# Pairs of up-projection chunks by seven products, and the down-projection in K=512 groups between them

## The chip, the core and the metric

The kernel runs on one core of one Trainium2 chip. The metric is the device time of one execution in microseconds. A time is the median of several runs; the profile shows one more execution, taken by the hardware profiler. TensorE (PE) multiplies, VectorE (DVE) and ScalarE (ACT) do the elementwise work, GpSimd (POOL) nearly nothing, and SyncE (SP) issues the transfers from main memory. Each works through its own queue in a fixed order.

## The reference

One layer of a hybrid decoder for 544 tokens (512 prompt, 8 x 4 sample), width 1024, in fp32. The change touches the output projection and what follows it:

```
merged = gates[:, :, 0] * ret_out + gates[:, :, 1] * conv_out + gates[:, :, 2] * xa_out
x = x + merged @ w_out                                   # 1024 x 1024
h2 = _rmsnorm(x, g_ffn)
x = x + jnp.square(jax.nn.relu(h2 @ w_up)) @ w_down      # 1024 x 4096, 4096 x 1024
y = _rmsnorm(x, g_final)
```

## The kernel before

An fp32 product is three matmuls of a rounded type: each factor is cast to a high part, the difference is the low part, and hi·hi, hi·lo and lo·hi are summed in a PSUM bank. Activations lie with channels on the 128 partitions and the 544 tokens along the free axis, in two halves of 272.

All projections go through one sequence of **chunks** (`seq`). A chunk is 128 output columns; with a depth of K=1024 it has 8 blocks of 128 x 3 products x 2 halves = 48 matmuls of 272 columns, with K=512 it has 24. `step(t)` issues the matmuls of chunk t (L200) into `pp`, a tile of two banks with two buffers, then `prep(t+2)`, which makes the weight parts of the chunk after next (ScalarE casts `whi` from `raw`, L177; VectorE forms `wlo`, through the helper at L102), then the evacuation of chunk t, then the functions posted for it by `at(key, d, fn)`, and last `load(t+4)`, which issues a DMA from SP into `raw` (two buffers, L166). A raw tile of K=1024 is 512 KB; a **half tile**, K=512, is 256 KB.

The sequence ends with: eight chunks of the output projection (**wo**), whose evacuation (`evac_out`) adds the input `xin` to give the residual `x1` and makes the high and low parts `h2h`, `h2l` of x1 times the gain; four **groups** of eight **up** chunks and eight **down** chunks (`dn`), where group g's down chunks take the 1024 channels that its up chunks have made (`ah`, `al`) and add into x1; in the fourth group the down chunks take only the first 512 channels, and 16 chunks of 12 matmuls (**last**) take the others, one half of the tokens at a time. The weights of last are resident: loaded early into `wres` (L850) and split by `resident`. In the end `final` sums the squares (`fsq`, `sq` into `fin`, L880 and L881) and the output is scaled.

`ffn_scale`, posted behind wo, makes `rs2` = 1/(mean square + eps), with a reciprocal of 544 columns on VectorE. `evac_up` uses it: r = max(p, 0) · rs2 and r · p on VectorE, then a cast on ScalarE and the low part on VectorE (`split`, L114 and L102).

What sets the order: the program is written step by step, and each engine's queue has its instructions in the order in which the code issues them.

Of the kernel before, what the change touches and what calls it, by code (L numbers as in the profile page):

```python
# [21 lines left out]
NB = 8  # L22
# [30 lines left out]
UPD3 = 1  # L53
PE_NS = dict(xa1=(4500, 3), xa2=(1100, 3), xa3=(4500, 3), xa4=(220, 1), ret_k=(1100, 3), ret_scores=(3200, 4),
# [12 lines left out]
class Builder:  # L67
    def __init__(self, ctx, tc, a, o):
        self.tc, self.nc, self.a, self.o = tc, tc.nc, a, o
        self.sb = ctx.enter_context(tc.tile_pool(name="sb", bufs=1))  # L70
        self.ps = ctx.enter_context(tc.tile_pool(name="ps", bufs=1, space=bass.MemoryType.PSUM))
# [6 lines left out]
        self.quota = 99  # L78

# [7 lines left out]
    def tmp(self, s, n=T, dt=F32):  # L87
        return self.sb.tile([P, n], dt, name=self.name(s), tag="T", bufs=NT)

    def small(self, s, dt=F32):  # L90
        return self.sb.tile([P, 2 * P], dt, name=self.name(s), tag="U", bufs=3)

    def const(self, s, shape, dt=F32):
        return self.sb.tile(shape, dt, name=s, tag=s)
# [59 lines left out]
    def load(self, t):  # L154
        if t >= len(self.chunks) or "parts" in self.chunks[t]:
            return
        w, idx = self.chunks[t]["w"]
        ks = self.chunks[t]["ks"]
        if w == "w_mem_kv" and idx % 6 > 1:
            if idx % 2 == 0:  # L160
                self.pair = self.sb.tile([P, 2, 2, 4, P], F32, name=self.name("raws"), tag="S8", bufs=2)
# [7 lines left out]
    def prep(self, t):  # L169
        if t >= len(self.chunks) or "parts" in self.chunks[t]:  # L170
            return
# [15 lines left out]

    def step(self, t):
        c = self.chunks[t]
        self.quota = c.get("quota", 99)  # L190
# [3 lines left out]
        xh, xl = c["rhs"]()  # L194
        n, nk = c["n"], 4 * len(c["ks"])
        for k in range(nk):
            wh, wl = parts[k // 4][0][:, k % 4], parts[k // 4][1][:, k % 4]
            for w, x in ((wh, xh), (wh, xl), (wl, xh)):
                for s in c["hs"]:
                    mm(pt[:, s, :n], w, x[:, 4 * c["ks"][0] + k, s * n:(s + 1) * n],  # L200
                       start=(k == 0 and w is wh and x is xh),
                       stop=(k == nk - 1 and w is wl))
        self.pe_ns += self.pe_cost(t)
        self.dve_ns = max(self.dve_ns, self.pe_ns)
        posts = self.posts.pop(t, [])
# [34 lines left out]
    # ---------------------------------------------------------------- memory keys and values  # L240
# [18 lines left out]
    # ---------------------------------------------------------------- memory attention  # L259
# [25 lines left out]
    def load_s8(self, src, key):  # L285
        t = self.sb.tile([P, 4, 2, 256], F32, name=self.name("s8"), tag="S8", bufs=2)
# [3 lines left out]
    def xa1(self, h):  # L290
# [15 lines left out]
        def tail():  # L306
            for w in range(2):
                self.load_s8(self.a["cmv"][h, w], ("v", w))
            mx = self.sb.tile([P, 6], F32, name=self.name("mx"), tag="mx", bufs=1)
            nm = self.sb.tile([P, 6], F32, name=self.name("nm"), tag="nm", bufs=1)  # L310
            sm = self.sb.tile([P, 6], F32, name=self.name("sm"), tag="sm", bufs=1)
            rs = self.sb.tile([P, 6], F32, name=self.name("rs"), tag="rs", bufs=1)
# [5 lines left out]
            p4 = self.sb.tile([P, 4, NM], F32, name=self.name("p"), tag="P5")  # L318
            ps = self.sb.tile([P, NM], F32, name=self.name("psm"), tag="OS")
# [34 lines left out]
    def xa3(self, h):  # L354
# [14 lines left out]
        def tail():  # L369
# [7 lines left out]
            self.os = self.sb.tile([P, 256], F32, name=self.name("os"), tag="OS")  # L377
# [25 lines left out]
    # ---------------------------------------------------------------- conv branch  # L403
# [6 lines left out]
    def evac_gt(self, c):  # L410
        def f(pt):
# [4 lines left out]
            e = self.sb.tile([P, EXT + SEQ + NB * XS], F32, name=self.name("ext"), tag="ext", bufs=2)  # L416
# [11 lines left out]
    def queue_conv(self, c, e, es):  # L428
# [14 lines left out]
        def sample():  # L443
            cwb = self.vecs[:, w0:w0 + CW].unsqueeze(1).to_broadcast([P, NB, CW])
            r = self.sb.tile([P, NS, NB], F32, name=self.name("cr"), tag="cr", bufs=1)
# [9 lines left out]
        def total():  # L455
            if c == 0:
                self.ysum = self.sb.tile([P, T], F32, name="ysum", tag="ysum")
# [10 lines left out]
    # ---------------------------------------------------------------- retention  # L468
# [48 lines left out]
    def stack_k(self, src):  # L517
        self.kdup = self.small("kdup").rearrange("p (c s) -> p c s", c=2)
        self.kcat = self.small("kcat", F32R).rearrange("p (c s) -> p c s", c=2)
        t = self.sb.tile([P, 2, TS], F32, name=self.name("ks"), tag="ks", bufs=1)  # L520
# [36 lines left out]
    def ret_k(self, h):  # L557
        b = self.to_tokens(self.kf, self.kcat)

        def tail():  # L560
# [5 lines left out]
            self.kst = self.sb.tile([P, 2, 256], F32R, name=self.name("kst"), tag="pk")  # L566
# [44 lines left out]
    def ret_intra_s(self, h):  # L611
# [6 lines left out]
        def tail():  # L618
            self.scs = self.sb.tile([P, P], F32, name=self.name("scs"), tag="scs")
# [3 lines left out]
    def ret_o(self, h):  # L623
# [16 lines left out]
        def tail():  # L640
            self.on = self.sb.tile([P, 4, 256], F32, name=self.name("on"), tag="P5")
            self.os = self.sb.tile([P, 256], F32, name=self.name("os"), tag="OS")
            st = self.sb.tile([P, 5, 6], F32, name=self.name("st"), tag="st", bufs=1)
            mv = self.sb.tile([P, 5, 2], F32, name=self.name("mv"), tag="mv", bufs=1)
            rs = self.sb.tile([P, 5], F32, name=self.name("rsg"), tag="rsg", bufs=1)
# [11 lines left out]
            nb = self.sb.tile([P, 5], F32, name=self.name("nb"), tag="nbg", bufs=1)  # L657
# [56 lines left out]
    # ---------------------------------------------------------------- tail of the mixer  # L714
# [19 lines left out]
    def ln_mean(self):  # L734
# [3 lines left out]
        def tail():  # L738
# [3 lines left out]
            self.vsum = self.sb.tile([P, T], F32, name="vsum", tag="ysum")  # L742
# [57 lines left out]
    def evac_out(self, j):  # L800
        def f(pt):
            if j == 0:
                self.x1 = self.big("x1", [P, NC8, T])
                self.h2h = self.big("h2h", [P, NC8, T], F32R)
                self.h2l = self.big("h2l", [P, NC8, T], F32R)
                self.ssq = self.sb.tile([P, T], F32, name="ssq", tag="ysum")
            self.tt(self.two(self.x1[:, j]), pt[:, :, :HALF], self.two(self.xin[j]), ALU.add)
            gf = self.vec("g_ffn", j)
            self.act(self.h2h[:, j], self.x1[:, j], AF.Copy, scale=gf)
            sq = self.ssq if j == 0 else self.tmp("sq")  # L810
            self.act(sq, self.x1[:, j], AF.Square)
            yield
            self.stt(self.h2l[:, j], self.x1[:, j], gf, self.h2h[:, j], ALU.mult, ALU.subtract)
            if j:
                self.tt(self.ssq, self.ssq, sq, ALU.add)
        return f

    def ffn_scale(self):
        b = self.mean_of(self.ssq)

        def tail():
            self.rs2 = self.sb.tile([P, T], F32, name="rs2", tag="cossin")
            for s in range(2):
                self.act(self.rs2[:, s * HALF:(s + 1) * HALF], b[s][:, :HALF], AF.Identity, bias=self.epsc)
            self.v("reciprocal", self.rs2, self.rs2)
            self.act(self.sb.tile([P, 1], F32, name="warm", tag="mx"), self.epsc, AF.Sqrt)
        return tail

    # ---------------------------------------------------------------- feed-forward
    def evac_up(self, g, k):  # L830
        def f(pt):
            if k == 0 and g == 0:
                self.ah = self.big("ah", [P, NC8, T], F32R)
                self.al = self.big("al", [P, NC8, T], F32R)
            r, t = self.tmp("r"), self.tmp("r2")
            ps = pt[:, :, :HALF]
            self.stt(self.two(r), ps, 0.0, self.two(self.rs2), ALU.max, ALU.mult)
            self.tt(self.two(t), ps, self.two(r), ALU.mult)
            yield from self.split(self.ah[:, k], self.al[:, k], t)
# [8 lines left out]
    def resident_load(self, j):  # L848
        self.wres[j] = self.tmp("wres", 512)
        self.nc.sync.dma_start(out=self.wres[j], in_=self.a["w_down"][24 + j][:, 4:8].rearrange("p k c -> p (k c)"))  # L850

    def resident(self, j):
        w = self.wres[j]
        if j == 0:
            self.rh = self.big("rh", [P, NC8, 4, P], F32R)
            self.rl = {}
        if j % 4 == 0:
            self.rl[j // 4] = self.sb.tile([P, 4, 4, P], F32R, name=self.name("rl"), tag="S8", bufs=2)

        return lambda: self.split(self.rh[:, j], self.rl[j // 4][:, j % 4], w.rearrange("p (k c) -> p k c", k=4))  # L860

    def evac_last(self, s, j):
        def f(pt):
# [5 lines left out]
            if j == 0:  # L869
                if s == 0:  # L870
                    self.fsqt = self.sb.tile([P, T], F32, name="fsq", tag="ysum")
# [39 lines left out]
    # ---------------------------------------------------------------- everything  # L911
    def build(self):
# [6 lines left out]
        memt = self.sb.tile([P, 2, D], F32, name="memt", tag="S8", bufs=2)  # L919
# [337 lines left out]
```

## Time and profile before

| | |
|---|---|
| median of 3 runs | 1159.74 us (1159.67 to 1160.41) |
| span of the profiled execution | 1157.8 us |
| TensorE matmul busy | 1144.7 us (99%), 9292 matmuls |
| VectorE busy | 765.5 us (66%), 1304 instructions |
| ScalarE busy | 450.9 us (39%), 885 instructions |
| mean granted TensorE clock | 0.998 of full |
| DMA | 142.6 MB, 123 GB/s |

The profile is of one execution and its span goes from the first to the last instruction; the runs' time holds something around it as well. A busy share is a mean over the whole span. The row of an instruction has its line in the code, the engine, the operation, output<-inputs by the program's names, and the shape.

### The profile page before, as it was taken

Reading aid. Unit: us, or ns where it says so; the run is one execution under the profiler, and the core shown is the slowest. Engines: PE = TensorE matmul, PEld = TensorE weight load, DVE = VectorE, ACT = ScalarE, POOL = GpSimd, SP = SyncE. Lnnn points to the kernel's source line nnn. Section 1 sums busy time; section 2 is a strip of 40 time slices with the busy share of each in tenths; the row PEclk is TensorE's granted clock in tenths of the full one; section 3 lists DMA queues with packets and bytes.
Section 4 is the critical chain, followed back from the end, with each engine's and each line's share of the span. In section 5 each row is a group of like instructions: output and inputs, shape, how many; then the busy total and the mean of one; then the engine's idle time right before and its main releaser. Section 6 shows DMA issues by size and latency. Waiting matters only on the chain.

```text
span 1157.8 us, 22201 instructions
## 1 busy us (share of the span) xinstructions
PE 1144.7 (99%) x9292; PEld 1120.3 (97%) x9292; DVE 765.5 (66%) x1304; ACT 450.9 (39%) x885; POOL 1.6 (0%) x8
## 2 busy tenths in 40 slices
PE   8999999999999999999999999999999999999996
PEld 8999999999999999999999999999999999999996
DVE  5747898568888988888764766565335435534656
ACT  7735653534343452334454623433223222222322
POOL 0000000000000000000000000000000000000000
PEclk9999999999999999999999999999999999999999
DMA  8555454442215422632522334322222222222402
GB/s 318 189 181 204 161 202 155 169 152 91 78 56 171 170 66 95 223 87 86 188 87 65 99 120 165 127 79 92 92 91 86 82 89 92 92 91 72 153 32 78
DMA packets 42804, 142.60 MB, mean 123 GB/s; under 512 B 4784, under 2 KB 11056, under 8 KB 39632
## 3 DMA queue, kind: packets, MB, share of 16 engines
q1 hardware_dynamic: 42416, 141.01, 36.0%
q8 instruction: 73, 1.20, 0.4%
q14 instruction: 27, 0.22, 0.1%
q10 hardware_dynamic: 288, 0.17, 0.1%
HBM read 126.17 MB, written 15.00 MB: 122 GB/s over the span
## 4 chain that ended last, share of the span: by engine, by line
PE 98%; DVE 1%; ACT 0%; DMA 0%; issue 0%; DVEq 0%; ACTq 0%
PE pp L200 87%; PE xo L365 1%; PE ro L637 1%; PE xs L302 1%; PE tk L551 1%; PE up L701 0%; PE rs L142 0%; PE rs L141 0%; PE rs L140 0%; PE ro L141 0%; PE ro L142 0%; PE ro L140 0%; DMA memt<-in_mem 0%; PE rst L141 0%; PE rst L142 0%; PE rst L140 0%
## 5 line engine op out<-in xcount | busy, mean ns | idle before, releaser
L102 DVE TENSOR_TENSOR wlo<-raw,whi 128x512 fp32r<-128x512 f32 x324 | 220.8, 690 | 280.1 <-ACT whi L177 258.2
L177 ACT CAST whi<-raw 128x512 fp32r<-128x512 f32 x324 | 198.5, 620 | 431.5 <-PE pp L200 403.3
L200 PE MATMUL pp<-hh,whi 128*128 128x272 f32 x1280 | 268.1, 291 | 0.0
L200 PE MATMUL pp<-hl,whi 128*128 128x272 f32 x1280 | 263.9, 288 | 0.0
L200 PE MATMUL pp<-hh,wlo 128*128 128x272 f32 x1280 | 263.3, 287 | 0.0
L200 PEld LDWEIGHTS pp<-hh,whi 128*128 128x128 f32 x1280 | 199.8, 188 | 6.3 <-issue 4.9
L200 PEld LDWEIGHTS pp<-hh,wlo 128*128 128x128 f32 x1280 | 201.1, 188 | 0.0
L200 PEld LDWEIGHTS pp<-hl,whi 128*128 128x128 f32 x1280 | 200.2, 188 | 0.0
L200 PE MATMUL pp<-h2h,whi 128*128 128x272 f32 x512 | 105.8, 288 | 0.0
L200 PE MATMUL pp<-h2l,whi 128*128 128x272 f32 x512 | 105.6, 287 | 0.0
L200 PE MATMUL pp<-h2h,wlo 128*128 128x272 f32 x512 | 105.4, 287 | 0.0
L200 PE MATMUL pp<-ah,whi 128*128 128x272 f32 x448 | 92.4, 288 | 0.0
L200 PE MATMUL pp<-al,whi 128*128 128x272 f32 x448 | 92.4, 288 | 0.0
L200 PE MATMUL pp<-ah,wlo 128*128 128x272 f32 x448 | 92.2, 287 | 0.0
L102 DVE SCALAR_TENSOR_TENSOR y<-ext,vecs,y 128x512 f32<-128x512 f32 x120 | 89.8, 748 | 2.9 <-ACT y L111 2.8
L102 DVE SCALAR_TENSOR_TENSOR odd<-ext,vecs,odd 128x512 f32<-128x512 f32 x112 | 83.6, 747 | 0.0
L200 PEld LDWEIGHTS pp<-h2l,whi 128*128 128x128 f32 x512 | 80.4, 188 | 0.0
L200 PEld LDWEIGHTS pp<-h2h,whi 128*128 128x128 f32 x512 | 80.2, 189 | 0.1
L200 PEld LDWEIGHTS pp<-h2h,wlo 128*128 128x128 f32 x512 | 80.1, 188 | 0.0
L200 PEld LDWEIGHTS pp<-al,whi 128*128 128x128 f32 x448 | 70.3, 188 | 0.0
L200 PEld LDWEIGHTS pp<-ah,whi 128*128 128x128 f32 x448 | 70.1, 189 | 0.0
L200 PEld LDWEIGHTS pp<-ah,wlo 128*128 128x128 f32 x448 | 70.1, 188 | 0.0
(248 smaller groups left out, 1598.0 us busy)
## 6 DMA issues: line engine op xcount, KB each, us to landing
raw<-in_w_in SPq DMA_DIRECT2D x80, 512.0 KB, 3.7
raw<-in_w_up SPq DMA_DIRECT2D x32, 512.0 KB, 3.5
raw<-in_w_down SPq DMA_DIRECT2D x24, 512.0 KB, 3.5
s<-in_cmk SPq DMA_DIRECT2D x8, 1024.0 KB, 6.7
s<-in_cmv SPq DMA_DIRECT2D x8, 1024.0 KB, 6.2
s<-in_st SPq DMA_DIRECT2D x8, 1024.0 KB, 6.0
out_sts<-s SPq DMA_DIRECT2D x16, 512.0 KB, 5.4
raws<-in_w_mem_kv SPq DMA_DIRECT2D x10, 512.0 KB, 5.9
```

The costliest lines, as they stand in the source:

```text
L102: return getattr(self.nc.vector, fn)(out, *args, **kw)
L177: self.nc.scalar.copy(hi, raw)
L200: mm(pt[:, s, :n], w, x[:, 4 * c["ks"][0] + k, s * n:(s + 1) * n], start=(k == 0 and w is wh and x is xh), stop=(k == nk - 1 and w is wl))
L302: mm(sc[2][32 * g:32 * g + 32, :NM], self.qsp[:, c, w, 32 * g:32 * g + 32], self.s8[("k", w)][:, g, c], start=(w == 0 and c == 0), stop=(w ...
L365: mm(ob[2][32 * g:32 * g + 32, :256], self.pm[:, nb, w, 32 * g:32 * g + 32], self.s8[("v", w)][:, g, nb], start=(w == 0 and nb == 0), stop ...
L551: self.nc.tensor.transpose(b[blk // 2][:, (blk % 2) * 256 + d * P:(blk % 2) * 256 + (d + 1) * P], full[d][:, blk * P:(blk + 1) * P], self. ...
L637: mm(out[32 * g:32 * g + 32], self.qsp[:, c, w, 32 * g:32 * g + 32], self.s8[("s", w)][:, g, c], start=False, stop=(w == 1 and c == 1), sk ...
```

## The change

**Seven products.** Of the 32 up chunks, the first four stay. The other 28 are computed in 14 pairs, u = 2 to 15. A pair's weights are four quarters: a11 and a12 are the two K halves of its first chunk, a21 and a22 of its second. The activations are four blocks too: two K halves times two token halves. The 2 x 2 block product is written with seven products m1 to m7 of 12 matmuls each (4 blocks x 3 products x one half) instead of eight. `evac_out` makes the activations: `z` is x1 times the gain in four blocks for two wo chunks, and `d` four combinations of them (VectorE), each with a high and a low part in `hs`. `weights()` makes the weights: six of the seven are split (cast on ScalarE, low part `sl` on VectorE) from a11, a12, a22 and from sums and differences of the quarters, and so is the seventh, a12 less one of them, updated in place; it is a generator of eleven units per pair. One unit is taken behind each of the first six products of a pair, and 2, 2, 1, 0 behind the four down chunks that follow. Up chunks take three each.

`pair_step` has three banks: p and q (the two of a `pp` tile) and r (a bank of another pool). The sums across products are made by adding in a bank or by VectorE:

```diff
+        s1, s2 = s12[:, :HALF], s12[:, HALF:]
+        product("m1", p, True)
+        self.nc.scalar.copy(s1, p)
+        self.units(1)
+        product("m6", q, True)
+        self.tt(s2, q, s1, ALU.add)
+        self.units(1)
+        product("m5", r, True)
+        self.run([lambda: self.prep(t + 2)])
+        self.units(1)
+        product("m7", q, False)
+        self.tt(s3, q, s1, ALU.add)
+        put(3, r, s3)
+        self.units(1)
+        product("m2", p, False)
+        put(0, p, None)
+        self.units(1)
+        product("m4", q, False)
+        put(2, q, s1)
+        self.units(1)
+        product("m3", r, False)
+        put(1, r, s2)
+        self.run([c["evac"]])
...
+        if t + 4 < len(self.chunks):
+            self.load(t + 4)
```

`put` writes a block of the result into z: block 0 by a relu on ScalarE, the others by an addition on VectorE. `evac_pair` then takes relu and square of z on ScalarE, and a cast and a low part of all four blocks, 1088 columns. In pairs 14 and 15 it multiplies z by rs2 before the cast.

The weights of one pair, with the loads of the next pair's quarters:

```diff
+            w["m1"] = self.wsplit(a11)
+            yield
+            self.tt(s3, a11, a21, ALU.subtract)
+            self.quarter(*((u + 1, 0)))
+            yield
+            self.tt(s2, a22, s3, ALU.subtract)
+            yield
+            w["m6"] = self.wsplit(s2)
+            yield
+            self.tt(a21, a21, a22, ALU.add)
+            yield
+            w["m5"] = self.wsplit(a21)
+            self.quarter(u + 1, 2)
+            yield
+            w["m7"] = self.wsplit(s3)
+            yield
+            w["m2"] = self.wsplit(a12)
+            yield
+            w["m4"] = self.wsplit(a22)
+            self.quarter(u + 1, 3)
+            yield
+            self.tt(a12, a12, s2, ALU.subtract)
+            yield
+            w["m3"] = self.wsplit(a12)
+            self.quarter(u + 1, 1)
+            yield
```

**Groups of half the depth.** Behind each pair stand four down chunks, D0 to D3, of K=512 (24 matmuls) for a group of 512 channels: eight groups, two pairs each, and the last group is `last`, with weights from the tail of `weights()` in place of wres.

```diff
-        for g in range(4):
-            if g < 3:
-                seq += [("up", g, k) for k in range(8)] + [("dn", g, j) for j in range(8)]
-        seq += [("up", 3, k) for k in range(5)] + [("dn", 3, j) for j in range(7)]
-        seq += [("up", 3, k) for k in range(5, 8)] + [("dn", 3, 7)]
+        seq += [("up", k) for k in range(4)]
+        for u in range(2, 16):
+            seq += [("pair", u)] + [("dn", u // 2 - 1, 4 * (u % 2) + j) for j in range(4)]
```

**The scale.** `evac_up` and `evac_pair` leave rs2 out. Instead x1 is multiplied by `v2` = mean square + eps during up chunks 1 to 3, and by rs2 after the down chunks of group 6; the last group's activations get rs2 as said. The reciprocal moves behind pair 4. In `evac_up` relu and square are on ScalarE:

```diff
-            self.stt(self.two(r), ps, 0.0, self.two(self.rs2), ALU.max, ALU.mult)
-            self.tt(self.two(t), ps, self.two(r), ALU.mult)
+            self.act(self.two(r), pt[:, :, :HALF], AF.Relu)
+            self.act(r, r, AF.Square)
...
+            if g == 6:
+                self.tt(self.x1[:, j], self.x1[:, j], self.rs2, ALU.mult)
...
+        at(("pair", 4), 0, self.invert)
```

**Memory.** SBUF is used in two phases: most tiles of the mixer lie in a pool that is closed at wo 0, where a pool for the feed-forward is opened; the xin loads of wo 0 and 1 are issued there. The rows of `w_up` are handed over in another order (blocks 0, 2, 4, 6, 1, 3, 5, 7).

On VectorE, in the stretch of down chunks behind a pair, the order before and the order now differ as follows. Before, at the end of a group's down chunks and the first up chunk of the next (names as above):

```order
L102 TENSOR_TENSOR wlo_1315_10146<-raw_1306_10034,whi_1314_10145 128x512 [waits DMAHW3_49,PE_49,Activation_49]
L102 TENSOR_TENSOR wlo_1317_10149<-raw_1306_10034,whi_1316_10148 128x512 [waits PE_49,Activation_49]
L102 TENSOR_TENSOR x1_1144_8667<-pp_1313_10096,x1_1144_8667 128x544
L102 TENSOR_TENSOR wlo_1321_10206<-raw_1312_10094,whi_1320_10205 128x512 [waits DMAHW4_49,PE_49,Activation_49]
L102 TENSOR_TENSOR wlo_1323_10209<-raw_1312_10094,whi_1322_10208 128x512 [waits PE_49,Activation_49]
L102 SCALAR_TENSOR_TENSOR r_1324_10213<-pp_1319_10156,rs2_9205 128x544
L102 TENSOR_TENSOR r2_1325_10214<-pp_1319_10156,r_1324_10213 128x544 [waits DVE_49]
L102 TENSOR_TENSOR al_1211_9212<-r2_1325_10214,ah_1210_9211 128x544 [waits Activation_49]
```

Now, from D2 behind a pair to the next pair's first sum (`rq` are the quarters, `sl` low parts, `s12` the tile of s1 and s2, the rest as above):

```order
L114 TENSOR_TENSOR rq_1420_10528<-rq_1420_10528,s2_1436_10630 128x512 [waits DVE_49]
L114 TENSOR_TENSOR sl_1461_10797<-rq_1420_10528,sh_1460_10796 128x512 [waits Activation_49]
L114 TENSOR_TENSOR x1_1144_8674<-pp_1464_10804,x1_1144_8674 128x544 [waits PE_49]
L114 TENSOR_TENSOR sl_1466_10831<-rq_1435_10615,sh_1465_10830 128x512 [waits DMAHW1_49,Activation_49]
L114 TENSOR_TENSOR wlo_1470_10862<-raw_1463_10802,whi_1469_10861 128x512 [waits DMAHW6_49,Activation_49]
L114 TENSOR_TENSOR x1_1144_8674<-pp_1468_10836,x1_1144_8674 128x544 [waits PE_49]
L114 TENSOR_TENSOR s3_1476_10885<-rq_1435_10615,rq_1444_10685 128x512 [waits DMAHW2_49]
L114 TENSOR_TENSOR s12_1474_10870<-pp_1472_10868,s12_1474_10870 128x272 [waits PE_49,Activation_49]
```

Between the low parts of two down chunks' weights there now stand a quarter's update and two low parts of the pair's weights, and the sum s2 of the next pair (`s12<-pp,s12`) has a low part, an addition into x1 and a difference ahead of it.

On SP the queue of loads in the same stretch was, before:

```order
L166 DMA raw_1276_9734<-in_w_down 128x1024 [waits DMAHW4_49,DVE_49]
L166 DMA raw_1282_9794<-in_w_down 128x1024 [waits DMAHW5_49,DVE_49]
L166 DMA raw_1288_9854<-in_w_down 128x1024 [waits DMAHW6_49,DVE_49]
L166 DMA raw_1294_9914<-in_w_down 128x1024 [waits DMAHW7_49,DVE_49]
L166 DMA raw_1300_9974<-in_w_up 128x1024 [waits DMAHW0_49,DVE_49]
L166 DMA raw_1306_10034<-in_w_up 128x1024 [waits DMAHW1_49,DVE_49]
L166 DMA raw_1312_10094<-in_w_up 128x1024 [waits DMAHW2_49,DVE_49]
L166 DMA raw_1318_10154<-in_w_up 128x1024 [waits DMAHW3_49,DVE_49]
```

Now, over one pair and its down chunks:

```order
L263 DMA rq_1477_10887<-in_w_up 128x512 [waits DMAHW1_49,DVE_49]
L263 DMA rq_1486_10957<-in_w_up 128x512 [waits DMAHW2_49,DVE_49]
L178 DMA raw_1489_10994<-in_w_down 128x512 [waits DMAHW7_49]
L263 DMA rq_1497_11034<-in_w_up 128x512 [waits DMAHW4_49,DVE_49]
L263 DMA rq_1503_11071<-in_w_up 128x512 [waits DMAHW5_49,DVE_49]
L178 DMA raw_1504_11073<-in_w_down 128x512 [waits DMAHW0_49]
L178 DMA raw_1508_11105<-in_w_down 128x512 [waits DMAHW3_49]
L178 DMA raw_1512_11137<-in_w_down 128x512 [waits DMAHW6_49,DVE_49]
```

Every load is of 128 x 512 now, and each pair has eight; the quarters a11, a21, a22 and a12 of the next pair (`rq`, in this order) stand between the half tiles of the down chunks (`raw`), and a12, which needs the buffer of its predecessor and so the update and the low part of that one, stands right ahead of the half tile for the next pair's D0.

## Rows read from the trace of the kernel before

**Rows 1.** The chain of waits, shares of the span by engine.

```profile
PE 98%; DVE 1%; ACT 0%; DMA 0%; issue 0%; DVEq 0%; ACTq 0%
```

**Rows 2.** Waits of TensorE: us in total, times, longest us.

```profile
PE mt L1043 <- DVE memt L102: 1.7, 2, 1.5
...
PE fin L881 <- ACT sq L111: 0.3, 1, 0.3
```

**Rows 3.** Busy time: us, PE, PEld, DVE, ACT, POOL; clock, DMA, GB/s.

```profile
767.75:1121.60 353.85, 353.85 (x2832) 353.85 (x2832) 171.24 (x251) 94.55 (x158) 0.00 (x0) 1.00 0.27 90
```

**Rows 4.** Pieces of the chain: start us, us, what.

```profile
767.74 367.58 PE pp L200 x2940
1136.23 10.66 PE pp L200 x84
```

**Rows 5.** VectorE by form: count, busy us, mean ns, idle before.

```profile
L102 DVE TENSOR_TENSOR wlo<-raw,whi 128x512 fp32r<-128x512 f32 x324 | 220.8, 690 | 280.1 <-ACT whi L177 258.2 <-PE up L701 13.0 <-PE rb L682 3.7
...
L102 DVE TENSOR_TENSOR al<-r,ah 128x544 fp32r<-128x544 f32 x32 | 23.2, 726 | 22.9 <-ACT ah L114 22.9
...
L102 DVE TENSOR_TENSOR x<-pp,x 128x544 f32<-128x544 f32 x32 | 23.0, 719 | 5.0 <-PE pp L200 4.9
...
L102 DVE TENSOR_TENSOR x<-pp,x 128x272 f32<-128x272 f32 x16 | 7.1, 442 | 4.1 <-PE pp L200 3.2
...
L102 DVE RECIPROCAL rs<-rs 128x544 f32<-128x544 f32 x1 | 3.6, 3553 | 0.3 <-ACT rs L111 0.3
```

**Rows 6.** ScalarE by form.

```profile
L177 ACT CAST whi<-raw 128x512 fp32r<-128x512 f32 x324 | 198.5, 620 | 431.5 <-PE pp L200 403.3 <-issue 7.6 <-DMA raw<-in_w_in 5.7
L111 ACT ACT_TABLE_LOAD x20 | 25.7, 1283 | 24.9 <-DVE nm L102 18.5 <-DVE y L102 4.5 <-PEq L1238 1.7
...
L111 ACT ACTIVATE sq<-x 128x272 f32<-128x272 f32 x14 | 6.1, 433 | 15.7 <-DVE x L102 15.7
...
L111 ACT ACTIVATE sq<-x 128x544 f32<-128x544 f32 x7 | 4.5, 643 | 0.0
```

**Rows 7.** Timeline: start us, duration us, engine, line; an up chunk.

```profile
901.63 0.72 DVE L102 TENSOR_TENSOR r<-pp,r 128x544 f32<-128x544 f32 x1
...
902.39 0.65 ACT L114 CAST ah<-r 128x544 fp32r<-128x544 f32 x1 [2.15 <-DVE r L102]
...
903.07 0.73 DVE L102 TENSOR_TENSOR al<-r,ah 128x544 fp32r<-128x544 f32 x1 [0.72 <-ACT ah L114]
...
903.71 0.69 DVE L102 TENSOR_TENSOR wlo<-raw,whi 128x512 fp32r<-128x512 f32 x1
```

**Rows 8.** Timeline: two chunks of last, and the final sum.

```profile
1122.98 0.29 PE L200 MATMUL pp<-ah,rl 128*128 128x272 f32 x1
...
1123.31 0.44 DVE L102 TENSOR_TENSOR x<-pp,x 128x272 f32<-128x272 f32 x1 [0.78 <-PE pp L200]
...
1147.93 0.73 PE L881 MATMUL fin<-sq,ones 128*128 128x272 f32 x2 [0.32 <-ACT sq L111]
```

**Rows 9.** DMA issues: count, KB each, median us to landing.

```profile
raw<-in_w_down SPq DMA_DIRECT2D x8, 256.0 KB, 2.7
```

**Rows 10.** DMA issues of 1083.7 to 1084.3.

```profile
wres<-in_w_down SPq DMA_DIRECT2D x1, 256.0 KB, 3.1
```

**Rows 11.** The tile wres, all eight loads.

```profile
DMA to landing us min/median/max: 2.9/3.6/4.5
```

**Rows 12.** Timeline: two loads and the cast of the first.

```profile
1083.36 0.33 SPq L166 DMA_DIRECT2D raw<-in_w_down  x1
...
1083.74 0.42 SPq L850 DMA_DIRECT2D wres<-in_w_down  x1
...
1086.27 0.62 ACT L177 CAST whi<-raw 128x512 fp32r<-128x512 f32 x1 [2.73 <-DMA raw<-in_w_down]
```

**Rows 13.** Busy time behind the last matmul, columns as above.

```profile
1151.00:1152.00 1.00, 0.00 (x0) 0.00 (x0) 0.96 (x4) 0.00 (x0) 0.00 (x0) 1.00 0.00 0
1152.00:1153.00 1.00, 0.00 (x0) 0.00 (x0) 1.00 (x4) 0.00 (x0) 0.00 (x0) 0.51 0.04 14
```

More of the change, by code (lines that the diff above doesn't have):

```diff
@@ L154, in load @@
     def load(self, t):
-        if t >= len(self.chunks) or "parts" in self.chunks[t]:
+        if t >= len(self.chunks) or "parts" in self.chunks[t] or "products" in self.chunks[t]:
             return
@@ L169, in prep @@
     def prep(self, t):
-        if t >= len(self.chunks) or "parts" in self.chunks[t]:
+        if t >= len(self.chunks) or "parts" in self.chunks[t] or "products" in self.chunks[t]:
             return
@@ L186, in pe_cost, with up_rhs, group_rhs, pair_step @@
         return len(c["hs"]) * len(c["ks"]) * 12 * (115 if c["n"] > 256 else 109)
+    def up_rhs(self, h, k, s):
+        return self.hs[k % 4][:, h, 2 * (k // 4) + s]
+    def group_rhs(self, g):
+        a = self.ag[g]
+        return lambda h, k, s: a[:, h, k, s * HALF:(s + 1) * HALF]
+    def pair_step(self, t):
+        c = self.chunks[t]
+        mm = self.nc.tensor.matmul
+        pt = self.ps.tile([P, 2, 512], F32, name=self.name("pp"), tag="pp", bufs=2)
+        p, q, r = pt[:, 0, :HALF], pt[:, 1, :HALF], self.bank("r")[:, :HALF]
+        wts, xs = c["products"](), c["slots"]()
+        def product(n, out, start):
+            wh, wl = wts[n]
+            for i in range(4):
+                for w, h in ((wh, 0), (wh, 1), (wl, 0)):
+                    mm(out, w[:, i], xs[i][:, h, SLOT[n]], start=(start and i == 0 and w is wh and h == 0),
+                       stop=(i == 3 and w is wl), skip_group_check=True)
+        s12, s3 = self.tmp("s12"), self.tmp("s3", HALF)
+        s1, s2 = s12[:, :HALF], s12[:, HALF:]
+        put = c["put"]
+        product("m1", p, True)
[20 more added lines that the diff above has]
+        self.run([c["evac"]])
+        self.run([f() for f, _, _ in self.posts.pop(t, [])])
+        self.pe_ns += 10500
+        self.dve_ns = max(self.dve_ns, self.pe_ns)
+        if t + 4 < len(self.chunks):
+            self.load(t + 4)
@@ new lines, in units, with quarter @@
+    def units(self, n):
+        for _ in range(n):
+            next(self.wgen, None)
+    def quarter(self, u, i):
+        if u < 16:
+            t = self.mx.tile([P, 4, P], F32, name=self.name("rq"), tag="rq%d" % i, bufs=1)
+            src = self.a["w_up"][2 * u + i // 2].rearrange("p (s k) c -> p s k c", s=2)[:, i % 2]
+        else:
+            t = self.mx.tile([P, 4, P], F32, name=self.name("rq"), tag="rq%d" % (i % 4), bufs=1)
+            src = self.a["w_down"][24 + i][:, 4:8]
+        self.nc.sync.dma_start(out=t, in_=src)
+        self.rq[(u, i)] = t
@@ L825, in tail, with scale_x, invert, act_tile @@
+            self.act(self.mx.tile([P, 1], F32, name="warm", tag="warm"), self.epsc, AF.Sqrt)
+        return tail
+    def scale_x(self, j):
+        def tail():
+            self.tt(self.x1[:, j], self.x1[:, j], self.v2, ALU.mult)
+        return tail
+    def invert(self):
+        def tail():
             self.v("reciprocal", self.rs2, self.rs2)
[L826 removed]
         return tail
[L830 to L839 removed]
+    def act_tile(self, g):
+        if g not in self.ag:
+            self.ag[g] = self.big("a", [P, 2, 4, T], F32R)
+        return self.ag[g]
@@ new lines, in evac_up, with put_pair, put @@
+    def evac_up(self, k):
+        def f(pt):
+            a = self.act_tile(0)
+            r = self.tmp("r")
+            self.act(self.two(r), pt[:, :, :HALF], AF.Relu)
+            self.act(r, r, AF.Square)
+            yield from self.split(a[:, 0, k], a[:, 1, k], r)
+        return f
+    def put_pair(self, u):
+        def put(i, src, add):
+            if i == 3:
+                self.z = self.mx.tile([P, 4, HALF], F32, name=self.name("z"), tag="Z", bufs=2)
+            d = self.z[:, ORDER[i]]
+            if add is None:
+                self.act(d, src, AF.Relu)
+            else:
+                self.tt(d, src, add, ALU.add)
+        return put
@@ new lines, in evac_pair, with f @@
+    def evac_pair(self, u):
+        def f():
+            z, a = self.z, self.act_tile(u // 2)
+            k = 2 * (u % 2)
+            self.act(z[:, 2:4], z[:, 2:4], AF.Relu)
+            self.act(z[:, 0], z[:, 0], AF.Relu)
+            self.act(z, z, AF.Square)
+            hi, lo = [a[:, h, k:k + 2].rearrange("p k (s t) -> p (k s) t", s=2) for h in range(2)]
+            if u > 13:
+                for i in range(2):
+                    self.tt(z[:, 2 * i:2 * i + 2], z[:, 2 * i:2 * i + 2], self.two(self.rs2), ALU.mult)
+            yield from self.split(hi, lo, z)
```

190 lines of the change are left out of this document (119 added, 71 removed).

## The prediction

> **What bounds the kernel now.** I read the chain of waits first. Its share by engine is 98% TensorE [rows 1], so the span is the length of TensorE's queue. The view of waits then says how often that queue stood still: five times in four groups, 3.6 us in all, of which the longest and the shortest group are shown [rows 2]; the longest is in the preparation of the inputs, the shortest in the last sums. In the feed-forward stretch from 767.75 to 1121.60 TensorE is busy for all 353.85 us with 2832 matmuls, VectorE for 171 us and ScalarE for 95 us [rows 3]. So one matmul of 272 columns costs 353.85 / 2832 = 0.125 us, and a matmul taken out there is worth 0.125 us, as long as the other engines keep pace. Where twelve matmuls in a row go into one bank, as in the products of the change, the rate is the same: 84 in 10.66 us with the drain of the last [rows 4].
>
> **The part that is certain: 168 matmuls go.** A pair of up chunks takes 2 x 48 = 96 matmuls now and 7 x 12 = 84 after, in 14 pairs; down chunks of half the depth take 24 instead of 48, but there are twice as many. 14 x 12 x 0.125 = 21.0 us. If TensorE never waited, the profiled span of 1157.8 us would become 1136.8. The median of the runs, 1159.74, stands 1.94 above the span, and I add that at the end.
>
> **What is added.** For one pair and its four down chunks D0 to D3 the VectorE order has 15 operations of 512 columns (11 for the pair's weights, 4 low parts of D0 to D3), 5 of 272, one of 1088 and 4 of 544. The prices are 0.69, 0.44, about 1.29 and 0.72 us [rows 5]; 1088 columns do not occur before, so I extend: 544 cost 0.726, 272 more cost 0.28 (0.719 less 0.442), hence 0.726 + 2 x 0.28 = 1.29; the bounds are twice the 544 row, 1.45, and 1.2. In sum 10.35 + 2.2 + 1.29 + 2.88 = 16.7 us, of 22.5 us of TensorE (84 + 4 x 24 matmuls). ScalarE has eleven casts of 0.62 and about 4 us of evacuation [rows 6], near 11 us. On shares both fit. What decides is the order, since each engine and the SP queue work strictly in theirs.
>
> **The loop that closes on itself.** I walk the order from the last matmul of one pair to that of the next, start to start. A dependent operation on another engine starts 0.04 after the end before it, an independent one on VectorE 0.08 before that end [rows 7]; VectorE starts 0.33 after the start of the last matmul of a group, which is 0.2 after its slot of 0.125 [rows 8].
> - After m3: 0.2; the last sum out of the bank (put 1, 272 columns) 0.48; on ScalarE the relu of it 0.47, the square of all 1088 columns 0.643 + 2 x 0.21 + 0.04 = 1.10 (0.21 is 0.643 less 0.433 [rows 6]), the cast 1.11 likewise from 0.65; back on VectorE the low part, 1.21 to the next start. VectorE stands still meanwhile. 4.57.
> - Six operations that queued behind it: low parts of D2, m2, m4 and D3 at 0.61, the additions into x1 of D0 and D1 at 0.64. 3.72.
> - a12 is updated in place (0.73), ScalarE casts it (0.66), VectorE takes the low part (0.72). 2.11.
> - Only now may SP fetch the next a12, and behind it in the same queue the half tile for the next pair's D0: 0.4 for the issue, then the landing. A half tile (256 KB) alone lands in 2.7 us [rows 9]; issued 0.38 behind another it took 3.1 [rows 10], and ScalarE starts about 0.1 after a landing [rows 12]. 3.6.
> - ScalarE casts that tile (0.66), VectorE takes its low part (0.61), adds D3 into x1 (0.64), forms s3 (0.61) and only then reads q for s2 (0.44, and 0.1 to TensorE). 3.06.
> - m7 writes into q, so it waits for that; m7, m2, m4, m3 take 6.0.
>
> 4.57 + 3.72 + 2.11 + 3.6 + 3.06 + 6.0 = 23.1 us, against 22.5 on TensorE. So m7 waits 0.6 us in each of 13 loops: 7.8 us. The least sure link is the landing. The tile view has 2.9 to 4.5 for the second of two [rows 11], and here a third load follows at once; the bounds of the loop are 22.6 (landing 2.7) and 24.4 (4.5), so 1 to 25 us in all; I take 3.1, since both of that pair are half tiles as here.
>
> [...]
>
> **Once only.**
> - The reciprocal of 544 columns (3.55 us on VectorE [rows 5]) leaves the first up chunk, where it cost TensorE nothing, and comes behind the low part of pair 4, inside the loop: 3.6 us. Bounds 0 and 3.6.
> - Pairs 14 and 15 multiply their result by rs2 on VectorE (two of 544, 1.45), and the x1 of group 6 gets one more multiplication per down chunk (0.76). In the loop of pair 14 that is 1.45 + 3 x 0.76 = 3.7; behind pair 15, where D2 waits for D0's bank, about 2. Bounds 0 and 8.
> - The output projection now makes z and d for the pairs: an odd step runs x1, h, low part, sum, four differences, copy of d (1.1), low part of d (1.2) and two weight halves in series, 8.1 us; an even one 4.5. That is 12.6 per two steps against 12.0, so x1 of its last chunk starts about 3.4 us after the chunk's end. From there to s2 of pair 2 VectorE has 18 operations at 0.61, 14 at 0.64 and 4.0 of others, 24.0 us, and waits some 5.6 on ScalarE (h 0.8, copy of d 1.1, v2 with its table load of 1.28 [rows 6] 2.1, two casts that must come back 1.6). TensorE gets there in 4 x 6.0 + 0.9 + 4.5 = 29.4. 3.4 + 29.6 - 29.4 = 3.6 us. Bounds 0 and 7.
>
> The new pool at the output projection makes xin loads issue one step later. They go out about 6 us before they are needed, after the last state stores have landed, so I cost them at nothing; if a store is late, VectorE's x1 is, by up to 2 us, which is within the bound of 7. Taking the reciprocal and the relu off the first up chunks gains nothing, since TensorE did not wait there.
>
> **Sum.** 7.8 + 3.6 + 5.7 + 3.6 = 20.7 us of new waits; 13 restarts at about 0.1 add 1.3. Span 1157.8 - 21.0 + 22.0 = 1158.8, time 1160.7, so 1161. The saving is real and is given back.
>
> **Rivals.**
> - Faster: the half tile lands as a lone one does, 2.7. Then the loop costs 1 us and the one-time costs remain: 1136.8 + 1 + 12.9 + 1.9 = 1152.6; without the start and pair 14 also, 1145. For it: the lone row; against: three loads within 0.8 us.
> - Slower, in one place: the half tile behind a12's load lands in 4 us, as the second load did behind a whole tile. The loop is 24.0, 13 x 1.5 = 19.5 instead of 7.8, time 1172. It decides from about 3.4 us on. For it: up to 4.5 in the trace [rows 11], and the third load; against: a third load shares the engines only after the second has begun.
> - Slower by the clock: the wait behind pair 4 leaves TensorE idle for 3.5 us. At the end of the trace its last work ends at 1148.66 (1147.93 + 0.73) [rows 8], the granted clock is still 1.00 until 1152 (2.4 GHz) and then 0.51 (1.2 GHz) [rows 13]. If the clock falls in that wait, some of the next matmuls take twice as long. No row shows how many; between none and the 36 up to the next down chunk's bank, 0 to 4.5 us: 1161 to 1165. The Trainium skill, "TensorE: Matmul & The Clock Gate", section "HAM oscillation", warns of such idle gaps; the trace agrees that idleness lowers the clock, and has no gap of this kind between matmuls.
> - That the change saves no matmuls is excluded: the order has 8064 such matmuls before and 7896 after.
>
> **How the numbers follow.** Forecast (landing near 3.1 to 3.3, 1157 to 1165) 0.47; faster rival 0.31 (1145 to 1156); late landing 0.15 (1166 to 1175); clock 0.07. The range 1150 to 1171 leaves out about a tenth at each side; the forecast's own is 1157 to 1165. A measurement here tells about 0.2%, 2.3 us, from no change: faster 0.31 and a little of the forecast, 0.34; same 0.28; slower 0.38.
>
> **What would show it.** In the profile after: TensorE's matmuls down by 168 at the same 0.125 us; waits of m7 (the second product into pp of a pair) on VectorE, 0.6 us in most pairs; VectorE's low part of D0 waiting some 3 us for ScalarE, and that for the DMA of raw; one wait of 3.5 us in the down chunks behind pair 4; 4 to 6 us of waits in the last two pairs. Without waits of m7, the landing was quicker than I take it. With VectorE never idle in front of that low part, the walk itself is wrong. A landing above 3.4 us makes it slower.

## The result and the profile after

The changed kernel takes 1205.28 us (median of 4 runs, 1200.61 to 1209.98) against 1159.91 before: a ratio of 1.0391, 95% interval 1.0358 to 1.0423. I had forecast 1161 and a range up to 1171, so it is 34 us above the range. The profiled execution has a span of 1206.6 us.

TensorE's busy time and share on the page, and the chain of waits by engine, answering to [rows 1]:

```profile
PE 1147.4 (95%) x9124; PEld 1111.1 (92%) x9124; DVE 845.8 (70%) x1458; ACT 520.3 (43%) x1004; POOL 1.6 (0%) x8
...
PE 74%; DVE 11%; ACT 7%; DMA 4%; issue 3%; SPq 0%; DVEq 0%; ACTq 0%
```

The 168 matmuls are gone (9292 less 9124), yet the chain now leaves TensorE for a quarter of the span. In the feed-forward stretch (columns as in [rows 3]):

```profile
767.75:1172.00 404.25, 357.70 (x2669) 345.87 (x2668) 243.81 (x388) 157.61 (x268) 0.00 (x0) 0.97 0.24 76
```

[rows 3] had 2832 matmuls in 353.85 us without a gap; here 2669 take 404.25. All of the loss is here: up to 767 us TensorE has done the same work in both traces (6265 and 6260 matmuls).

TensorE's waits (us in total, times, longest us), the first four groups, answering to [rows 2]:

```profile
PE pp L218 <- ACT s L225: 25.6, 14, 3.3
PE pp L218 <- DVE s L114: 7.5, 14, 0.5
PE pp L218 <- ACT z L123: 6.8, 14, 0.5
PE pp L327 <- DVE x L114: 6.1, 3, 3.3
```

L218 is the line of the products and L225 the copy of s1. Fourteen times each: three waits in every pair. The first matmuls behind these waits in one pair, from the timeline (idle time and releaser in brackets):

```profile
902.39 0.52 PE L218 MATMUL pp<-hs,sh 128*128 128x272 f32 x2 [2.03 <-ACT s L225]
...
909.25 0.52 PE L218 MATMUL pp<-hs,sh 128*128 128x272 f32 x2 [0.53 <-DVE s L114]
...
911.52 0.52 PE L218 MATMUL pp<-hs,sh 128*128 128x272 f32 x2 [0.49 <-ACT z L123]
```

The first follows twelve matmuls of m1, so it is m6, not m7. The second is m2 (it waits for s3), the third m4 (it waits for the relu of put 0). m7, which I had expected to wait, begins at 906.93 without any. None of the three needs what it waits for: m6 writes into q and the copy reads p; m2 adds into p and s3 reads q; m4 adds into q and the relu reads p. p and q are the two banks of one `pp` tile.

The chain of waits from one pair's a12 to the next pair's m6 (start us, us, what) shows what makes the first of them long:

```profile
925.11 0.33 SPq L263
...
925.49 3.31 DMA raw<-in_w_down
...
928.88 0.62 ACT whi L189
929.50 0.29 ACT s L225
...
929.84 1.26 PE pp L218 x8
```

SP issues a12's load at 925.11 and the half tile for the next D0 at 925.49; ScalarE casts it, and behind that cast in ScalarE's queue stands the copy s1, for which m6 waits.

The clock falls behind some of these waits. Here are four microseconds each around or after the ends of the waits at 790.17, 818.55, 866.03, 902.39, 982.25 and 1144.80 (columns as above; the granted clock is the third number from the end):

```profile
790.70:794.70 4.00, 4.00 (x22) 4.00 (x22) 3.17 (x6) 0.62 (x1) 0.00 (x0) 0.57 0.62 197
818.00:822.00 4.00, 3.45 (x16) 3.45 (x17) 2.18 (x4) 1.02 (x3) 0.00 (x0) 0.57 0.37 104
865.70:869.70 4.00, 3.67 (x17) 3.70 (x18) 3.26 (x7) 0.69 (x2) 0.00 (x0) 0.57 0.22 66
903.50:907.50 4.00, 4.00 (x22) 4.00 (x21) 2.84 (x5) 0.62 (x1) 0.00 (x0) 0.57 0.39 131
981.90:985.90 4.00, 3.65 (x17) 3.65 (x18) 2.38 (x5) 0.82 (x3) 0.00 (x0) 0.57 0.38 118
1145.60:1149.60 4.00, 4.00 (x22) 4.00 (x21) 3.10 (x6) 1.36 (x3) 0.00 (x0) 0.57 0.51 145
```

Each costs TensorE 0.43 x 4 = 1.7 us, 10.3 us together: most of each stretch ran at 1.2 instead of 2.4 GHz.

### The profile page after: what moved, and what is told of

It is laid out like the page before. It is cut to its first block, busy times and chain, and to the rows that moved or that the text cites. A ratio compares the mean times of both kernels' runs of the same rounds, so it can differ in the third digit from the quotient of the medians.

```text
span 1206.6 us, 22138 instructions
## 1 busy us (share of the span) xinstructions
PE 1147.4 (95%) x9124; PEld 1111.1 (92%) x9124; DVE 845.8 (70%) x1458; ACT 520.3 (43%) x1004; POOL 1.6 (0%) x8
## 4 chain that ended last, share of the span: by engine, by line
PE 74%; DVE 11%; ACT 7%; DMA 4%; issue 3%; SPq 0%; DVEq 0%; ACTq 0%
PE pp L327 51%; PE pp L218 8%; DMA raw<-in_w_down 4%; PE r L218 4%; DVE x L114 3%; ACT z L123 2%; DVE sl L114 2%; DVE wlo L114 2%; ACT a L126 1%; ACT whi L189 1%; ACT sh L269 1%; DVE rq L114 1%; DVE z L114 1%; DVE s L114 1%; PE xo L493 1%
## 5 line engine op out<-in xcount | busy, mean ns | idle before, releaser
L327 PE MATMUL pp<-a,whi 128*128 128x272 f32 x896 | 150.6, 291 | 6.1 <-DVE x L114 6.1
L218 PE MATMUL pp<-hs,sh 128*128 128x272 f32 x560 | 116.2, 303 | 40.0 <-ACT s L225 25.6
L218 PEld LDWEIGHTS pp<-hs,sh 128*128 128x128 f32 x560 | 89.9, 194 | 49.4 <-ACT s L225 28.7
L327 PEld LDWEIGHTS pp<-a,whi 128*128 128x128 f32 x896 | 127.0, 190 | 8.2 <-issue 5.1
L327 PE MATMUL pp<-a,wlo 128*128 128x272 f32 x448 | 92.9, 290 | 0.0
L218 PE MATMUL pp<-hs,sl 128*128 128x272 f32 x280 | 82.5, 294 | 0.0
L114 DVE TENSOR_TENSOR sl<-rq,sh 128x512 fp32r<-128x512 f32 x78 | 52.3, 686 | 38.8 <-ACT sh L269 38.7
L327 PEld LDWEIGHTS pp<-a,wlo 128*128 128x128 f32 x448 | 70.4, 190 | 0.0
L218 PEld LDWEIGHTS pp<-hs,sl 128*128 128x128 f32 x280 | 54.5, 195 | 0.0
L327 PE MATMUL pp<-memhl,whi 128*128 128x256 f32 x256 | 47.6, 286 | 0.9 <-DVE memhl L114 0.5
```

What stands on the lines that cost most here:

```text
L114: return getattr(self.nc.vector, fn)(out, *args, **kw)
L218: mm(out, w[:, i], xs[i][:, h, SLOT[n]], start=(start and i == 0 and w is wh and h == 0), stop=(i == 3 and w is wl), skip_group_check=True)
L327: mm(pt[:, s, :n], w[i], x(h, k, s), start=(k == 0 and i == h), stop=(k == nk - 1 and i == 1))
```

## The experiments

Theory A had two parts: the framework that places the waits sees p and q as one tile, so that each product waits for the readers of the other bank too; and the half tile's landing, behind a12 on SP, reaches TensorE through ScalarE's queue. The rivals were that the waits stand for late weights of these products, and that the landing is slow wherever it stands.

**Separate banks.** Only the tile changes:

```diff
-        pt = self.ps.tile([P, 2, 512], F32, name=self.name("pp"), tag="pp", bufs=2)
-        p, q, r = pt[:, 0, :HALF], pt[:, 1, :HALF], self.bank("r")[:, :HALF]
+        p, q, r = self.bank("p")[:, :HALF], self.bank("q")[:, :HALF], self.bank("r")[:, :HALF]
```

> The changed kernel, but with p and q in a PSUM tile of their own each (as r has one) instead of being the two halves of one pp tile; no other instruction is changed. Theory A: in the trace of the changed kernel the products m6, m2 and m4 of each pair wait for a reader of the OTHER half of their tile (m6 into q for the copy s1 out of p, m2 into p for the sum s3 out of q, m4 into q for the relu out of p), which they don't need. Then those three waits vanish in all 14 pairs (25.6, 7.5 and 6.8 us), the loop closes later, at m7, with a wait of 0.6 to 1.5 us per pair, and the time is 1160 to 1168. Rival B: the waits stand for the weights of those products, which ScalarE and VectorE make late; then nothing changes: 1200 to 1210.

Measured: 1170.12 us, ratio 1.0089 (1.0072 to 1.0106). The three waits are gone and m7's is there:

```profile
PE q L217 <- DVE s L114: 13.0, 13, 2.1
PE pp L326 <- DVE x L114: 6.1, 3, 3.3
```

The first holds the waits of pair 2 (2.13) and pair 15 (2.05) and eleven between of 0.33 to 1.53, in the mean 0.80. Rival B would have kept the three waits. The edit also frees the pair's `pp` buffer, but the waits of the down chunks for a buffer (for x1, 6.1 us) are the same as in the change. The time is 2 us above what I had written: three spells of half clock (5.1 us) were not in it. So the dependency on the shared tile is shown, and the loop that is left is the one of the prediction. Its chain from m7 to m7:

```profile
893.34 1.78 PE q L217 x12
...
899.71 0.45 DVE z L114
...
901.79 1.11 ACT a L126
...
904.74 0.72 DVE x L114
...
907.90 0.61 DVE rq L114
...
909.96 0.33 SPq L262
...
910.34 3.34 DMA raw<-in_w_down
...
913.75 0.63 ACT whi L189
...
915.73 0.96 DVE s L114 x2
...
916.74 0.39 PE q L217
```

893.34 to 916.74 is 23.4 us; the prediction's sum was 23.1.

**The half tile ahead of a12.** Its load is issued one step of the queue earlier, with the tile shared as in the change:

```diff
         self.run([lambda: self.prep(t + 2)])
+        early = c.get("units") == 2 and t > self.index[("pair", 2)] and "products" not in self.chunks[t + 4]
+        if early:
+            self.load(t + 4)
         jobs = [lambda: c["evac"](pt)]
...
-            if t + ahead < len(self.chunks) and self.chunks[t + ahead]["ahead"] == ahead:
+            if not early and t + ahead < len(self.chunks) and self.chunks[t + ahead]["ahead"] == ahead:
```

> The changed kernel, but on SP the half tile of the next pair's D0 is issued ahead of the load of a12 instead of behind it. Theory A (the landing of that half tile closes the loop, since the copy s1 stands behind its cast on ScalarE): the wait of ScalarE for raw of 3.9 to 5.0 us per pair goes, m6 waits some 0.5 us only (copy of s1, still needed by the shared tile), m2 and m4 wait as before: 14 x 2.3 = 32 us of waits, 1175 to 1183 in all. Rival B: the landing is late because the transfers are slow, not because of the place in the queue: 1198 to 1210.

Measured: 1185.77 us, ratio 1.0223 (1.0208 to 1.0238), 3 us above what I had written. Behind pair 2, m6 still waits in each pair, but for the copy alone:

```profile
945.56 0.52 PE L219 MATMUL pp<-hs,sh 128*128 128x272 f32 x2 [0.47 <-ACT s L226]
...
950.86 0.52 PE L219 MATMUL pp<-hs,sh 128*128 128x272 f32 x2 [0.53 <-DVE s L115]
...
953.13 0.52 PE L219 MATMUL pp<-hs,sh 128*128 128x272 f32 x2 [0.49 <-ACT z L124]
```

The load of the half tile is now issued at 938.83, 4.6 us before m1 starts, against 1.3 us in the change (925.49 and 926.81). ScalarE's waits for half tiles between 790 and 1110 us, in the change and here:

```profile
ACT whi L189 <- DMA raw<-in_w_down: 48.2, 11, 4.9
...
ACT whi L190 <- DMA raw<-in_w_down: 8.6, 16, 1.0
```

The period, from one m6 to the next, is 25.00 us (the next m6 starts at 970.56). So the place in the queue made the landing late. The 1.49 us of listed waits are not the price: without these waits (next run) the period is 22.7, so they cost 2.3 per pair. Each also ends a run of matmuls with a drain (the last matmul shows 0.29 us, its slot is 0.125) and begins one with a slower pair (0.52 instead of 0.41 for two), 0.27 us more for each of the three.

**Both.** The edits of the two runs before.

> Both edits: p and q in tiles of their own, and the half tile of D0 ahead of a12 on SP. Theory A: TensorE waits in no pair but 2, 4 and 14 or 15 (start, reciprocal, rs2 multiplications: 8 to 12 us in all), so 1136.8 + 8 to 12 + 1.9 = 1147 to 1151: faster than before. If there is a third limit in the loop (VectorE's own order), 1155 to 1165.

Measured: 1155.48 us (10 runs), ratio 0.9968 (0.9958 to 0.9977): faster than before, by a third of a per cent. No product waits but m7 in pair 2:

```profile
PE pp L326 <- DVE x L114: 7.6, 3, 3.3
...
PE q L217 <- DVE s L114: 2.1, 1, 2.1
```

TensorE's chain runs through a pair and its down chunks without a break:

```profile
929.94 1.50 PE p L217 x12
...
940.50 12.15 PE pp L326 x96
952.65 1.51 PE p L217 x12
```

The pair started at 929.94 and the next at 952.65, so the period is 22.71: the 22.5 of 180 matmuls and 0.2. The time is 4.5 us above the top of what I had written. The waits that are left, three of 7.6 us together for x1 and that of m7, lie within the 8 to 12 us expected; not expected were two spells of half clock, at 854 and at 1110 us (some 1.7 us each).

**The other part of the change alone.** Groups of K=512, phases, scale and reciprocal as changed, but two plain up chunks in place of each pair:

```diff
-            seq += [("pair", u)] + [("dn", u // 2 - 1, 4 * (u % 2) + j) for j in range(4)]
+            seq += [("up", 2 * u), ("up", 2 * u + 1)] + [("dn", u // 2 - 1, 4 * (u % 2) + j) for j in range(4)]
```

(With it, `weights()` makes only the resident weights of last, and `evac_up` takes rs2 in the last four up chunks.)

> Only the other part of the change: groups of 512 channels with down chunks of K=512 between, the two SBUF phases, the moved scale and reciprocal, z and d in the output projection; but each pair is two plain up chunks of 48 matmuls from raw weights, with no products, quarters or weight sums. Both theories: 8064 matmuls as before, TensorE nearly without waits, 1158 to 1164. If the rearrangement itself costs something (the reciprocal, the start of the new phase, half tiles), 1165 to 1180.

Measured: 1161.66 us (10 runs), ratio 1.0015 (1.0005 to 1.0024). The rearrangement costs about 2 us (the trace has one wait of 2.4 us for x1 in its last group, with a spell of half clock). The other 44 us of the change are in the pairs, net of the 21 that their missing matmuls save.

**Without rs2.** A scale common to all channels of a token cancels in the final norm, if its eps is scaled too. On the kernel of the two edits:

```diff
-            self.nc.scalar.copy(self.rs2, self.v2)
+            self.act(self.rs2, self.v2, AF.Square, scale=EPS ** 0.5)
...
-            self.act(r, b[:, :HALF], AF.Sqrt, bias=self.epsc)
+            self.tt(r, b[:, :HALF], self.rs2[:, sl], ALU.add)
+            self.act(r, r, AF.Sqrt)
...
-        at(("pair", 4), 0, self.invert)
```

The multiplications by rs2 in `evac_pair` and `evac_down` go too.

> e3_both without rs2: the reciprocal behind pair 4, the multiplications of z in pairs 14 and 15 and of x1 in group 6 go, and the final norm adds eps times v2 squared (one operation on ScalarE early, one of 272 columns on VectorE per half at the end) instead of eps, since a scale of all channels of a token cancels there. If the three waits for x1 that e3_both has left (3.34, 1.39 and 2.83 us, 7.6 in all) and the two spells of half clock behind them (2 x 1.7) are these steps' price: 7.6 + 0.9 of restarts + 3.4 - 0.5 at the end = 11.4 us less, 1144 (1142 to 1147). If the waits come from elsewhere: 1152 to 1156.

Measured: 1146.21 us, ratio 0.9887 (0.9872 to 0.9901), 9.3 us less than with both edits (11.4 forecast). The trace has no spell of half clock before the end. Of the 7.6 us of waits for x1, 0.3 are left:

```profile
PE q L217 <- DVE s L114: 2.2, 1, 2.2
...
PE pp L326 <- DVE x L114: 0.3, 1, 0.3
```

**The scaling spread.** Six of the eight multiplications by v2 go where VectorE stands still in pairs 2 and 3:

```diff
+            if u in (2, 3):
+                for j in range(4 * u - 8, 4 * u - 5):
+                    self.scale_x(j)()
             yield from self.split(hi, lo, z)
...
-        for j in range(8):
-            at(("up", 1 + j // 3), 0, self.scale_x, j)
+        for j in (3, 7):
+            at(("up", 1 + j // 4), 0, self.scale_x, j)
```

(v2 has a tile of its own here.)

> e4_norecip, and six of the eight multiplications of x1 by v2 move from up chunks 1 to 3 into the stretches of pairs 2 and 3 where VectorE stands still while ScalarE takes relu, square and cast of z. If the wait of m7 in pair 2 (2.1 us in e3_both) is VectorE's backlog from these steps, 6 x 0.72 = 4.3 us earlier: the wait goes, 2.1 to 2.3 us less than e4_norecip, about 1142. If it is the chain through the first norm and its table load, no difference.

Measured: 1144.98 us, ratio 0.9873 (0.9857 to 0.9890): 1.2 us less, not 2.2, and the intervals of the two runs overlap.

```profile
PE pp L326 <- DVE x L114: 1.0, 1, 1.0
PE q L217 <- DVE s L114: 1.0, 1, 1.0
```

The wait of m7 in pair 2 went from 2.2 to 1.0 us and a wait for x1 from 0.3 to 1.0. So about half of m7's wait seems to have been VectorE's backlog; what holds the other half I did not settle. This version is the best: 15 us faster than before, 60 faster than the change.

**The copy first.** The changed kernel, but the cast and low part of the next D0's weights are issued behind s1 and s2:

```diff
-        self.run([lambda: self.prep(t + 2)])
+        if not (t + 1 < len(self.chunks) and "products" in self.chunks[t + 1]):
+            self.run([lambda: self.prep(t + 2)])
...
         self.tt(s2, q, s1, ALU.add)
+        self.run([lambda: self.prep(t + 1)])
```

> The changed kernel, tile shared and a12 ahead of the half tile on SP as in it, but the cast and low part of the next D0's half tile are issued behind the copy s1 (ScalarE) and the sum s2 (VectorE) of the pair, instead of ahead of them. Theory A: m6 waits long only because its copy stands on ScalarE behind a cast that waits for the landing; the landing itself may stay as late as it is, since D0 needs its weights some 10 us later. m6 then waits 0.5 us in each pair, m2 and m4 as before, a period of 25.0 us as in e2_early, and 1180 to 1188. Rival: the late landing holds the pair in another way too (VectorE's low part ahead of m5 or m7, SP's queue): a period of 26 us and more, 1195 to 1210.

Measured: 1184.81 us, ratio 1.0215 (1.0198 to 1.0232).

```profile
PE pp L218 <- ACT s L225: 8.6, 14, 2.4
PE pp L218 <- DVE s L114: 7.5, 14, 0.6
PE pp L218 <- ACT z L123: 6.8, 14, 0.5
```

As expected by theory A: the load is as late as in the change (issued at 941.17, 1.3 us before m1 at 942.51), and m6's waits fall from 25.6 to 8.6 us, since its copy no longer stands behind the cast. Moving the load or moving the cast does the same (1185.77 and 1184.81).

## Why the prediction was wrong, step by step

The mechanism that I named as the danger, the loop through a12, the landing and VectorE, is there, and its length was nearly right (23.4 against 23.1). The step that failed is its last one: "m7 writes into q, so it waits for that; m7, m2, m4, m3 take 6.0." I let only true dependencies between p, q and their readers hold up TensorE. The program has a wait of m6, m2 and m4 for the reader of the other bank. It stood in the order that could be read beforehand, as the first matmuls of m6, m2 and m4 of one pair in the changed kernel:

```
L218 MATMUL pp_1430_10596<-hs_1145_8676,sh_1398_10377 128x272 [waits Activation_49]
L218 MATMUL pp_1430_10596<-hs_1145_8676,sh_1410_10483 128x272 [waits DVE_49]
L218 MATMUL pp_1430_10596<-hs_1145_8676,sh_1412_10487 128x272 [waits Activation_49]
```

The three are released by the copy s1 out of p, the sum s3 out of q and the relu out of p. The prediction names none of these waits: it puts them at nothing, without a reason. With tiles of their own m6 has no wait, m2 waits for ScalarE (s1 out of p) and m4 for VectorE (s3 out of q), and neither holds TensorE up.

Two things follow from it. First, 2.3 us in each period, even where nothing is late. Second, the loop closes at m6 in place of m7: behind the cast come the copy (0.34 us to the start of m6) and then six products instead of four, with the two short waits among them, and the period is 25.8 to 30.0 (m6 at 929.84 and 955.65; at 845.82 and 875.81, where the reciprocal lies between), in the mean (1144.80 - 790.17) / 13 = 27.3.

A second term was mis-sized, the landing. The half tile behind a12 took 3.2 to 4.3 us in the 13 loops of the change (median 3.8), not 3.1. Apart from that the walk was right. Take the predicted loop of 23.06 us and put each measured landing in the place of 3.1: with separate banks eight of the nine loops without a spell of half clock or a step of rs2 come out within 0.11 us. One of them, with 23.06 + 4.18 - 3.1 = 24.14 against 988.41 - 964.17 = 24.24:

```profile
964.17 0.52 PE L217 MATMUL q<-hs,sh 128*128 128x272 f32 x2 [1.01 <-DVE s L114]
...
981.17 4.18 DMA raw<-in_w_down
...
988.41 0.52 PE L217 MATMUL q<-hs,sh 128*128 128x272 f32 x2 [1.25 <-DVE s L114]
```

With the shared tile the same terms give 23.06 less 2.40 (low part, D3's addition, s3, s2), plus 0.34 for the copy, 3.0 for m6 and m5 and 1.56 for the two waits with their drains: 25.6 from m6 to m6 at a landing of 3.1. For the loop from 955.65 that makes 25.6 + 4.03 - 3.1 = 26.5, and it took 26.6:

```profile
955.65 0.52 PE L218 MATMUL pp<-hs,sh 128*128 128x272 f32 x2 [1.26 <-ACT s L225]
...
977.19 4.03 DMA raw<-in_w_down
...
982.25 0.82 PE L218 MATMUL pp<-hs,sh 128*128 128x272 f32 x2 [2.08 <-ACT s L225]
```

Seven loops agree so. Four that begin with a spell of half clock take 1.5 to 1.6 us more, and the two with rs2's steps in them 3.5 and 3.1 more.

By the spans, the 69.8 us above the 1136.8 of a TensorE that never waits part as follows:

| piece | from | us | in the prediction |
|---|---|---|---|
| late half tile, with the tile shared | 1206.6 - 1183.0 | 23.6 | 7.8 at m7, without the tile |
| shared tile alone | 1183.0 - 1153.6 | 29.4 | 0 |
| rs2: reciprocal and multiplications | 1153.6 - 1143.9 | 9.7 | 3.6 + 5.7 = 9.3 |
| the rest (start of the pairs, 0.2 in each period, ends) | 1143.9 - 1136.8 | 7.1 | 3.6 + 1.3 |

The pieces are not independent: the late half tile costs 23.6 with the tile shared and 1166.9 - 1153.6 = 13.3 without, against the 7.8 + 1.3 of restarts that I gave it; longer landings and the clock make the difference. That the row of rs2 meets its 9.3 is in part luck: the waits for x1 went down by 7.3 us, and two spells of half clock, which were not in the sum, went with them.

Point by point:
- 168 matmuls less at 0.125: right. With nothing in the way a pair with its down chunks takes 22.71 us, 0.2 more than 180 x 0.125.
- The reciprocal, 3.6: the trace has one wait of 3.34 us for x1 behind pair 4. Right, but the clock then fell, 1.7 more.
- Pairs 14 and 15, 5.7: with both edits the waits for x1 there are 1.39 and 2.83 us, 4.2 together. Right in place, a little high.
- The start, 3.6: the first wait of pair 2 is 3.00 in the change, 2.1 with both edits. Near.
- Landing at 3.1: 3.3 is the median of all half tiles behind the pairs, but those behind a12, which close the loop, took 3.8. Too low by 0.6 us, some 8 us over 13 loops, and past the 3.4 that I had named as the point where it gets slower. My sign for it misled: I wrote that without waits of m7 the landing was quicker. There are none, because m6 waits first, and the landing was slower.
- The clock, a rival at 0.07 with one place and up to 4.5 us: six places of 1.7 us. I priced it as a side case of one wait, while the length of that wait was itself the unknown. The Trainium skill, "TensorE: Matmul & The Clock Gate", section "HAM oscillation", has a kernel that pays for it in every round of its loop; here the clock fell at six of the waits, as the rows above show.
- The slower rival, a landing of 4 us, 1172, at 0.15: the right place, sign and nearly size of the landing, but its price rested on the same wrong end of the loop. With separate banks, where that end is right, the time is 1170.12. So without the shared tile my 1161 would still have been 9 us too low, by the longer landings and three spells of the clock.

The Trainium skill, "PSUM — Partial Sum Buffer", section "PSUM bank collisions raise a hardware error", has the rule to guard PSUM by bank (and quadrant), not by address. p and q are different banks, so by that rule m6 needs no guard against a reader of p. The runs agree: with a tile for each bank the waits of m6, m2 and m4 are gone, and 35 us with them (1205.28 to 1170.12). The guard in the change is by tile, which is coarser than the rule.

## What to carry to other kernels

Whoever writes and reads two banks in turn should give each its own tile: in this kernel two halves of one tile were one object to the waits, and a reader of the one half stopped the writer of the other. When a change's order is read beforehand, each wait of the engine that bounds has to be assigned to the instruction that releases it, and the queue in front of that instruction looked at, down to its DMA; the waits that the forecast put at nothing are where it failed. A load that is needed soon does not belong in a queue behind one that waits for a buffer.

## What the runs showed of the hardware

A short wait of TensorE costs more than the view of waits lists: 1.49 us listed in a pair cost 2.3 us of period. A half tile that is issued 0.4 us behind another load landed in 3.2 to 4.3 us in the change, where a lone one took 2.7 before.

The clock did not fall only at the one long wait that I had looked at: in the change it fell at all six waits of 2.03 to 3.34 us, for a stretch at 0.5 that cost 1.7 us each, and at none of those up to 1.99. The length of the wait does not decide it alone, though. In pair 2 of four other runs the clock stayed up: at a wait of 2.10 us (both edits), of 2.20 (without rs2), of 2.41 (the copy first) and of 3.01, which ends at 790.59 (the half tile ahead of a12):

```profile
790.60:794.60 4.00, 4.00 (x32) 4.00 (x33) 3.75 (x7) 1.08 (x2) 0.00 (x0) 1.00 0.58 187
```

What decides it was not settled. The four runs of the changed kernel spread over 9 us, those of the kernel before over 1. Their mean granted clocks, 0.996, 0.993, 0.989 and 0.986, fall in the order in which their times rise, so the number of such stretches is the likely reason; it was not shown.
